# Two modulation products moved to ScalarE and GpSimd, and the weight stream put in another order

## The chip, the cores and the metric

The kernel runs on one core of a Trainium2 chip. The core has engines with a program each, which wait for one another by semaphores: TensorE (PE in the profile; PEld is its weight load), VectorE (DVE), ScalarE (ACT), GpSimd (POOL) and SyncE (SP), which issues the DMA transfers. The metric is the device time of one execution in microseconds (us), as the median of three runs.

## The reference

Two blocks of a transformer are computed in f32 for 256 tokens of width 1024. Only the start of the first block bears on this change. Each half layer is modulated by a vector c:

```python
def ada_modulation(c, w, b):
    m = jax.nn.silu(c) @ w + b            # w: 1024 x 3072
    shift, scale, gate = jnp.split(m[:, None, :], 3, axis=-1)
    return shift, scale, 1.0 + gate
...
shift, scale, gate = ada_modulation(c, ada_w[layer, 0], ada_b[layer, 0])
h = x * (1.0 + scale) + shift
y = mixer_ab(h, ...)                      # a window attention and an indexed (top-64) attention
x = layer_norm(DN_ALPHA * x + gate * y, ...)
shift, scale, gate = ada_modulation(c, ada_w[layer, 1], ada_b[layer, 1])
h = x * (1.0 + scale) + shift
y = squared_relu_mlp(h, ...)
```

So the first gate is needed when mixer_ab is done, and the shift and scale of the second half layer directly after the first layer norm.

## The kernel before, in words

All weights pass through one stream (class Stream): a list of items, mostly 128 x 2048 f32 (1 MB), which SyncE loads in the order of the list into four `raw` buffers, up to three items ahead. An item is then worked off in pieces, which the program puts between the other work (`pump`, `need`, `get`). A weight item's pieces split it into a high part `whi` (ScalarE, L157) and a low part `wlo` (VectorE, L158). An item of modulation weights has two pieces of 128 x 1024. `S.hold(key, a, b, behind)` lets the pieces of some items be issued only behind a named instruction, here the last one of `select`.

The first half layer (mixer_ab) goes as follows. VectorE makes shift and scale of the first half layer (items ada00). TensorE projects the tokens; VectorE adds up index scores for two tiles t of 128 tokens (index_scores: seven L913 steps of 128 x 128 for t = 0, seven of 128 x 256 for t = 1). `select` finds the 64 best keys of each query by rounds of MAX8 (L925) and MATCH_REPLACE8 (L928), and makes a mask of them (L933 to L947). The attention units follow, first six with that mask (ub), then six with the window mask (ua): scores on TensorE (L490, L496), a maximum on VectorE (L498), exponentials on ScalarE (L509), a division on VectorE (L526), a transpose (L534, L536) and the product with the values. The output projection by `ab_w_out` (items about) ends in the layer norm, whose inverse root is taken on GpSimd (L258).

The first gate (items ada00g) is made on TensorE: `ada_products` multiplies 32 equal columns of silu(c) with four strips of 256 columns, eight times over (L444), into one PSUM bank, and `ada_gate` adds the bias and spreads the row over the partitions (L452, L457, L459). Shift and scale of the second half layer (items ada (1, 0) to (1, 7)) are made on VectorE: sixteen multiplications of 128 x 1024 with a summed output (`ada_piece`, L436; tile junk).

The order of the instructions on each engine is fixed when the program is built, by the program's own order and a scheduler; each engine then works through its list in that order and waits at an instruction that isn't ready.

Of the kernel before, what the change touches and what calls it, by code (L numbers as in the profile page):

```python
# [8 lines left out]
F32 = DT.float32  # L9
# [4 lines left out]
AF = mybir.ActivationFunctionType  # L14
# [5 lines left out]
KT = 8  # L20
# [176 lines left out]
class Kern:  # L197
# [241 lines left out]

    def ada_products(self, raw, ps, kt, o, n):  # L440

        def pc():
            for g in range(4):
                self.nc.tensor.matmul(ps()[32 * g:32 * g + 32, 0:n], self.ccol[:, kt, :],  # L444
                                      raw[:, o + g * n:o + g * n + n], start=kt == 0, stop=kt == KT - 1)
        return pc

    def ada_gate(self, ps, gate):

        nc = self.nc  # L450
        row = self.pa.tile([128, 256], F32, tag="grow", name="grow", bufs=1)
        nc.vector.scalar_tensor_tensor(row, ps[:, 0:256], 1.0, self.gate_b, op0=ALU.add, op1=ALU.add)  # L452
        for h in range(2):
            p = self.ps("o")
            for q in range(2):
                g = 32 * (2 * h + q)
                nc.tensor.matmul(p[:, q * 256:q * 256 + 256], self.ident[:, g:g + 1].to_broadcast([128, 128]),  # L457
                                 row, start=True, stop=True)
            nc.scalar.activation(gate[:, h * 512:h * 512 + 512], p, AF.Copy, scale=1.0 / ALPHA)  # L459
# [295 lines left out]
    def mixer_ab(self, gate, early):  # L755
# [3 lines left out]
        for i in range(2):  # L759
# [8 lines left out]
        nc.scalar.activation(e, self.col("c", 0, 8), AF.Sigmoid)  # L768
        self.ccol = self.pa.tile([128, KT, 32], F32, tag="ccol", name="ccol")
        nc.gpsimd.tensor_tensor(self.ccol, self.col("c", 0, 8)[:, :, None].to_broadcast([128, KT, 32]),  # L770
                                e[:, :, None].to_broadcast([128, KT, 32]), op=ALU.mult)
        self.gate_b = self.pa.tile([128, 256], F32, tag="gate_b", name="gate_b")

# [12 lines left out]
        for kt in range(KT):  # L786
# [19 lines left out]
            for t in range(2):  # L806
                k = kt % 4
                self.mm(p0[t][:, :456], (xT[:, kt, t * 128:t * 128 + 128],), wt, slice(k * 456, k * 456 + 456),
                        kt == 0, kt == KT - 1)

        cqT = self.pa.tile([128, 2, 256], F32, tag="cqT", name="cqT", bufs=1)
# [30 lines left out]
        def ropeT(src, qT, name):  # L842
# [9 lines left out]
            return qT  # L852

        def keysT(src, kT):

            nc.gpsimd.memset(kT[0:64, :, 1, :], 0.0)
            nc.gpsimd.memset(kT[64:128, :, 0, :], 0.0)
            p = self.ps("o")
            for j in range(2):
                for t in range(2):  # L860
                    nc.tensor.transpose(p[:, j * 256 + t * 128:j * 256 + t * 128 + 128],
                                        src[t][:, j, :, :].rearrange("p a d -> p (a d)"), self.ident)
            for r in range(2):
                hs = slice(64 * r, 64 * r + 64)
                nc.scalar.activation(kT[hs, :, r, :], p[hs, :].rearrange("p (a b) -> p a b", a=2), AF.Copy)
# [9 lines left out]
        for t in range(2):  # L875
# [7 lines left out]
            iw.append(w_)  # L883
        kTb = self.px.tile([128, 2, 2, 256], F32, tag="tm", name="kTb", bufs=8)
        keysT(kd, kTb)
        iqT = self.px.tile([128, 4, 256], F32, tag="tm", name="iqT", bufs=8)
# [119 lines left out]
        self.cst_late()  # L1006
        for g in range(4):
            nc.sync.dma_start(self.gate_b[32 * g:32 * g + 32, :],
                              A["rows"][ROWS["gate_b"]:ROWS["gate_b"] + 1, 256 * g:256 * g + 256].to_broadcast([32, 256]))
        for t in range(2):  # L1010
            select(t, sc[t])
        S.hold(("ada00g", 0), 4, 16, [self.sel_last[1]])
        acc = [[None, None], [None, None]]

        kTa = self.px.tile([128, 2, 2, 256], F32, tag="tm", name="kTa", bufs=8)
        aqT = qTs[:, 0:4, :]

# [38 lines left out]
        def hook(i):  # L1056
            if i == 0:
                window()
                S.need(S.index["ada00g", 3])
            if i == 5:  # L1060
                self.ada_gate(self.strips, gate)
            if i == 11:
# [557 lines left out]
    def schedule_items(self):  # L1620
# [14 lines left out]

        def strips():

            if self.strips is None:
                self.strips = self.ps("acc")
            return self.strips  # L1640
        self.strips = None

        def gate0(j):
            def fn(raw):
                return [self.ada_products(raw, strips, 2 * j + q, 1024 * q, 256) for q in range(2)]
            S.add(("ada00g", j), A["ada"][8 + j], 2048, fn=fn)

        def ada(i, j):
            acc, mod = self.adas[i]

            def fn(raw):
                if j < 8:
                    ps = [self.ada_piece(raw, 0, acc, j), self.ada_piece(raw, 1, acc, 8 + j)]
                else:
# [7 lines left out]
        for j in range(4):  # L1662
            gate0(j)
        for j in range(4):
            S.add(("about", (j + 2) % 4), A["ab_w_out"][(j + 2) % 4], 2048, f32=j >= 2)
            ada(1, 2 * j)
            ada(1, 2 * j + 1)
        ex = {}
# [295 lines left out]
```

## Time and profile before

| | us |
|---|---|
| median of 3 runs | 1337.09 (1335.97 to 1338.56) |
| the profiled execution | 1336.42 |
| its span, from first to last instruction | 1334.5 |
| index scores and select | 52.2 to 78.7 |
| the ub units up to the fifth exponential | 81.0 to 98.9 |
| the rest of mixer_ab | 98.9 to 134.5 |
| inverse roots of the first layer norm | from 142.56 and from 152.29 |
| the first one of the second layer norm | from 331.73 |

The page gives busy times of each engine, the chain of waits that ended last, and the costliest groups of instructions. Times in rows are microseconds from the span's start; a duration in a row of the timeline includes a start-up that overlaps the instruction before it, so consecutive VectorE instructions may overlap by some 0.07 us. An f32 matmul shows as two rows.

### The profile page before, as it was taken

How to read it: one execution, taken by the hardware profiler on the slowest of the kernel's cores; microseconds unless marked ns; L12 is line 12 of the kernel's file. 1: busy time of each engine (PE TensorE's matmuls, PEld its weight loads, DVE VectorE, ACT ScalarE, POOL GpSimd, SP SyncE). 2: the span in 40 equal slices, each digit the busy share in tenths (PEclk: the TensorE clock that was granted, in tenths of full speed). 3: DMA queues.
4: the chain of work that ended last, by engine and by line, in shares of the span. 5: the costliest groups of instructions: out<-in, count | busy, mean ns of one | idle time of the engine just before them, and what ended most of it. 6: DMA issues, size and time to landing. Idle time of an engine off the chain costs nothing.

```text
span 1334.5 us, 18965 instructions
## 1 busy us (share of the span) xinstructions
PE 1289.8 (97%) x6970; PEld 1051.4 (79%) x6970; DVE 1006.6 (75%) x2048; ACT 708.1 (53%) x1532; POOL 43.8 (3%) x74
## 2 busy tenths in 40 slices
PE   5899999999999999999999999999999999999997
PEld 2356688888787788888699988888888877888886
DVE  7789999976999698666798778666677555766664
ACT  3245645554566665555543437555566754755552
POOL 2000000000100000000010000000000000000000
PEclk9999999999999999999999999999999999999999
DMA  9639689974457468555343334555534333455530
GB/s 363 252 146 332 248 299 347 343 272 158 180 202 281 158 217 300 188 191 178 109 158 116 138 127 170 188 185 188 189 139 158 126 127 126 174 189 189 190 127 32
DMA packets 39023, 260.21 MB, mean 195 GB/s; under 512 B 4625, under 2 KB 5009, under 8 KB 9362
## 3 DMA queue, kind: packets, MB, share of 16 engines
q1 hardware_dynamic: 38786, 258.47, 53.8%
q8 instruction: 55, 0.90, 0.3%
q0 software_dynamic: 144, 0.52, 0.1%
q14 instruction: 38, 0.31, 0.1%
HBM read 257.93 MB, written 1.05 MB: 194 GB/s over the span
## 4 chain that ended last, share of the span: by engine, by line
PE 73%; issue 11%; DVE 8%; ACT 3%; DMA 3%; POOL 2%; SPq 0%; POOLq 0%; DVEq 0%; ACTq 0%
PE acc L229 11%; PE acc L227 11%; PE acc L228 11%; PE scr L250 6%; PE o L250 6%; PE scr L251 3%; PE o L251 3%; PE scr L496 3%; PE acc L234 2%; DVE wlo L158 2%; DMA raw<-in_ada_dram 2%; PE o L534 1%; PE scr L229 1%; DVE junk L436 1%; POOL sm L258 1%
## 5 line engine op out<-in xcount | busy, mean ns | idle before, releaser
L158 DVE TENSOR_TENSOR wlo<-raw,whi 128x512 fp32r<-128x512 f32 x724 | 471.2, 686 | 129.8 <-ACT whi L157 119.9
L157 ACT ACTIVATE whi<-raw 128x512 fp32r<-128x512 f32 x724 | 418.9, 626 | 211.3 <-PE acc L229 87.7
L227 PE MATMUL acc<-whi,hh 128*128 128x512 f32 x512 | 201.2, 394 | 0.0
L228 PE MATMUL acc<-wlo,hh 128*128 128x512 f32 x512 | 201.2, 393 | 0.0
L229 PE MATMUL acc<-whi,hl 128*128 128x512 f32 x512 | 200.1, 392 | 0.0
L250 PE MATMUL scr<-xT,whi 128*128 128x512 f32 x464 | 166.8, 398 | 0.0
L250 PE MATMUL o<-xT,whi 128*128 128x512 f32 x464 | 166.1, 397 | 0.0
L251 PE MATMUL o<-xT,wlo 128*128 128x256 f32 x464 | 130.5, 281 | 0.0
L251 PE MATMUL scr<-xT,wlo 128*128 128x256 f32 x464 | 130.4, 281 | 0.0
L227 PEld LDWEIGHTS acc<-whi,hh 128*128 128x128 f32 x512 | 96.2, 188 | 22.9 <-ACT hh L737 1.3
L229 PEld LDWEIGHTS acc<-whi,hl 128*128 128x128 f32 x512 | 96.2, 188 | 22.1 <-DVE hl L738 0.8
L436 DVE SCALAR_TENSOR_TENSOR junk<-raw,csil 128x1024 bf16<-128x1024 f32 x88 | 108.6, 1234 | 6.2 <-DMA raw<-in_ada_dram 5.8
L228 PEld LDWEIGHTS acc<-wlo,hh 128*128 128x128 f32 x512 | 96.2, 188 | 18.6
L250 PEld LDWEIGHTS o<-xT,whi 128*128 128x128 f32 x464 | 87.1, 188 | 21.0
L250 PEld LDWEIGHTS scr<-xT,whi 128*128 128x128 f32 x464 | 87.1, 188 | 20.7 <-issue 0.5
L251 PEld LDWEIGHTS scr<-xT,wlo 128*128 128x128 f32 x464 | 87.5, 189 | 2.7 <-issue 0.5
L251 PEld LDWEIGHTS o<-xT,wlo 128*128 128x128 f32 x464 | 87.6, 189 | 0.0
L737 ACT ACTIVATE hh<-f 128x512 fp32r<-128x512 f32 x58 | 36.7, 633 | 86.8 <-DVE f L736 86.7
L731 ACT ACTIVATE r<-scr 128x256 f32<-128x256 f32 x58 | 22.3, 384 | 96.6 <-PE scr L251 96.6
L732 DVE TENSOR_TENSOR r<-scr,r 128x256 f32<-128x256 f32 x58 | 24.6, 424 | 55.7 <-ACT r L731 55.4
L738 DVE TENSOR_TENSOR hl<-f,hh 128x512 fp32r<-128x512 f32 x58 | 40.1, 691 | 33.3 <-ACT hh L737 33.1
L229 PE MATMUL acc<-whi,xT 128*128 128x512 f32 (+1 forms) x176 | 63.4, 361 | 0.7 <-DVE xT L306 0.5
(398 smaller groups left out, 2294.9 us busy)
## 6 DMA issues: line engine op xcount, KB each, us to landing
raw<-in_m_w_dram SPq DMA_DIRECT2D x128, 1024.0 KB, 4.8
raw<-in_ada_dram SPq DMA_DIRECT2D x48, 1024.0 KB, 5.4
raw<-in_c_qk_dram SPq DMA_DIRECT2D x8, 1024.0 KB, 4.9
raw<-in_h_qf_dram SPq DMA_DIRECT2D x8, 1024.0 KB, 4.8
raw<-in_mla_o_dram SPq DMA_DIRECT2D x8, 1024.0 KB, 4.8
raw<-in_c_v_dram SPq DMA_DIRECT2D x4, 1024.0 KB, 4.7
raw<-in_c_w_out_dram SPq DMA_DIRECT2D x4, 1024.0 KB, 4.8
raw<-in_h_i_dram SPq DMA_DIRECT2D x4, 1024.0 KB, 5.0
```

The source lines that it names most:

```text
L157: nc.scalar.activation(hi, raw[:, a:b], AF.Copy)
L158: nc.vector.tensor_tensor(lo, raw[:, a:b], hi.bitcast(F32), op=ALU.subtract)
L227: mm(ps, xh, wh, start=start, stop=False)
L228: mm(ps, xh, wl, start=False, stop=False)
L229: mm(ps, xl, wh, start=False, stop=stop)
L234: self.nc.tensor.matmul(ps, x[0], w(c), start=start, stop=stop)
L250: mm(ps.rearrange("p (a b) -> p a b", a=2), w.h(c), x, start=start, stop=False)
L251: mm(ps[:, n:2 * n], w.l(c), x[:, 0, :], start=False, stop=stop)
L436: nc.vector.scalar_tensor_tensor(junk, raw[:, j * 1024:(j + 1) * 1024], 1.0, self.csil, op0=ALU.mult, op1=ALU.mult, accum_out=acc[:, n:n + 1])
L496: nc.tensor.matmul(o, q, k, start=False, stop=(i == len(ops) - 1))
L737: nc.scalar.activation(hh, f, AF.Copy)
L738: nc.vector.tensor_tensor(hl, f, hh.bitcast(F32), op=ALU.subtract)
```

## The change

The first gate: ScalarE multiplies each 1 MB half by a column of silu(c) (128 x 1024, tile prod, two buffers), and GpSimd adds the product to the tile gate, eight times. `gate` starts as 1/32 on 32 partitions and zero elsewhere, with the bias loaded into its first row. Two matmuls with a matrix of ones sum it over the partitions. The TensorE strips, their PSUM bank and the VectorE step of `ada_gate` go.

The second half layer's shift and scale: GpSimd multiplies (128 x 1024, into the same two buffers prod), and ScalarE sums along the row. The sixteen L436 instructions of VectorE for items ada (1, 0) to (1, 7) go; those of other layers stay.

The stream's order: the eight items ada (1, j) now come directly after the gate's four and ahead of the four about items, where they were interleaved before. The hold begins at the first about item. The memsets of the key tiles are issued earlier.
```diff
-    def ada_products(self, raw, ps, kt, o, n):
+    def ada_rows(self, raw, kts):
+        nc = self.nc
+        def piece(q, kt):
+            def pc():
+                w = self.prod[kt % 2]
+                nc.scalar.activation(w, raw[:, q * 1024:q * 1024 + 1024], AF.Identity, scale=self.ccol[:, kt:kt + 1])
+                nc.gpsimd.tensor_tensor(self.grow, self.grow, w, op=ALU.add)
+            return pc
+        return [piece(q, kt) for q, kt in enumerate(kts)]
+
+    def ada_piece2(self, raw, j, acc, n):
+        nc = self.nc
         def pc():
-            for g in range(4):
-                self.nc.tensor.matmul(ps()[32 * g:32 * g + 32, 0:n], self.ccol[:, kt, :],
-                                      raw[:, o + g * n:o + g * n + n], start=kt == 0, stop=kt == KT - 1)
+            w = self.prod[j]
+            nc.gpsimd.tensor_tensor(w, raw[:, j * 1024:(j + 1) * 1024], self.csil, op=ALU.mult)
+            nc.scalar.activation(w, w, AF.Copy, accum_out=acc[:, n:n + 1])
         return pc
-    def ada_gate(self, ps, gate):
-        row = self.pa.tile([128, 256], F32, tag="grow", name="grow", bufs=1)
-        nc.vector.scalar_tensor_tensor(row, ps[:, 0:256], 1.0, self.gate_b, op0=ALU.add, op1=ALU.add)
+    def ada_gate(self, gate):
         for h in range(2):
             p = self.ps("o")
-            for q in range(2):
-                g = 32 * (2 * h + q)
-                nc.tensor.matmul(p[:, q * 256:q * 256 + 256], self.ident[:, g:g + 1].to_broadcast([128, 128]),
-                                 row, start=True, stop=True)
+            nc.tensor.matmul(p, self.ones, self.grow[:, h * 512:h * 512 + 512], start=True, stop=True)
             nc.scalar.activation(gate[:, h * 512:h * 512 + 512], p, AF.Copy, scale=1.0 / ALPHA)
...
+        self.grow = gate
+        self.prod = [self.pa.tile([128, 1024], F32, tag="prod", name="prod"), self.tm("prod")]
+        for a, b, v in ((0, 32, 0.0), (32, 64, 1.0 / 32), (64, 128, 0.0)):
+            nc.gpsimd.memset(gate[a:b, :], v)
...
-        S.hold(("ada00g", 0), 4, 16, [self.sel_last[1]])
+        S.hold(("about", 2), 0, 16, [self.sel_last[1]])
...
+        S.need(S.index["ada00g", 3])
...
-                S.need(S.index["ada00g", 3])
+            if i == 3:
+                S.need(S.index["ada", 1, 7])
             if i == 5:
-                self.ada_gate(self.strips, gate)
+                self.ada_gate(gate)
...
-                    ps = [self.ada_piece(raw, 0, acc, j), self.ada_piece(raw, 1, acc, 8 + j)]
+                    f = self.ada_piece2 if i == 1 else self.ada_piece
+                    ps = [f(raw, 0, acc, j), f(raw, 1, acc, 8 + j)]
...
+        for j in range(8):
+            ada(1, j)
         for j in range(4):
             S.add(("about", (j + 2) % 4), A["ab_w_out"][(j + 2) % 4], 2048, f32=j >= 2)
-            ada(1, 2 * j)
-            ada(1, 2 * j + 1)
```

Three places show what moves. On GpSimd, between the memsets of the key tile kTa and the two inverse roots of the first layer norm (L258), nothing stood before:
```order
L258 TENSOR_TENSOR sm_317<-rsq_318,mhalf 128x1
L856 MEMSET kTa 64x2x256
L857 MEMSET kTa 64x2x256
L258 TENSOR_TENSOR sm_1284<-rsq_1285,mhalf 128x1
L258 TENSOR_TENSOR sm_1339<-rsq_1340,mhalf 128x1
```

Now the eight additions to gate and the sixteen multiplications with csil (silu(c) spread over the partitions) stand there, the first and the last of each shown:
```order
L869 MEMSET kTa 64x2x256
L448 TENSOR_TENSOR gate<-gate,prod 128x1024
L448 TENSOR_TENSOR gate<-gate,prod_171 128x1024
...
L448 TENSOR_TENSOR gate<-gate,prod_171 128x1024
L458 TENSOR_TENSOR prod<-raw_607,csil 128x1024
L458 TENSOR_TENSOR prod_171<-raw_607,csil 128x1024
...
L458 TENSOR_TENSOR prod_171<-raw_804,csil 128x1024
L258 TENSOR_TENSOR sm_1270<-rsq_1271,mhalf 128x1
L258 TENSOR_TENSOR sm_1325<-rsq_1326,mhalf 128x1
```

GpSimd's twenty-four new instructions all stand ahead of the layer norm's inverse roots, and they take prod's two buffers in turn.

On ScalarE, from the last index scores (rl) to the first exponentials (pt), the list before was:
```order
L907 ACTIVATE rl_455<-scr_453 128x512
L907 ACTIVATE rl_461<-scr_459 128x512
L851 ACTIVATE hT<-o_491 128x4x128
L851 ACTIVATE hT<-o_503 128x4x128
L509 ACT_TABLE_LOAD
L509 ACTIVATE pt_613,sm_614<-scr_605,sm_611 128x128 x4
```

Now (from the same index scores on; adaacc is the sum's column):
```order
L923 ACTIVATE rl_463<-scr_461 128x512
L447 ACTIVATE prod<-raw_340,ccol 128x1024
L447 ACTIVATE prod_171<-raw_340,ccol 128x1024
...
L459 ACTIVATE prod,adaacc_89<-prod 128x1024
L459 ACTIVATE prod_171,adaacc_89<-prod_171 128x1024
...
L864 ACTIVATE hT<-o_493 128x4x128
L864 ACTIVATE hT<-o_505 128x4x128
L459 ACTIVATE prod_171,adaacc_89<-prod_171 128x1024
L459 ACTIVATE prod,adaacc_89<-prod 128x1024
L518 ACT_TABLE_LOAD
L518 ACTIVATE pt_633,sm_634<-scr_625,sm_631 128x128 x4
L459 ACTIVATE prod_171,adaacc_89<-prod_171 128x1024
```

Five sums (L459), each of which waits for a GpSimd multiplication, now stand ahead of the first exponentials, and the sixth directly behind them.

On ScalarE around the fifth ub unit's exponentials (pt_818 before, pt_853 now), before and then now:
```order
L536 ACTIVATE pT_801<-o_796 128x512
L509 ACTIVATE pt_788,sm_789<-scr_781,sm_786 128x256 x2
L272 ACTIVATE oT_807<-o_776 128x4x128
L509 ACTIVATE pt_818,sm_819<-scr_811,sm_816 128x256 x2
L536 ACTIVATE pT_831<-o_826 128x512
```

```order
L459 ACTIVATE prod,adaacc_89<-prod 128x1024
L545 ACTIVATE pT_836<-o_831 128x512
L459 ACTIVATE prod_171,adaacc_89<-prod_171 128x1024
L459 ACTIVATE prod,adaacc_89<-prod 128x1024
L272 ACTIVATE oT_842<-o_760 128x4x128
L459 ACTIVATE prod_171,adaacc_89<-prod_171 128x1024
L518 ACTIVATE pt_853,sm_854<-scr_846,sm_851 128x256 x2
```

The last of the sixteen sums stands directly ahead of the fifth unit's exponentials, so eleven of them lie between the first and the fifth unit's. The split of the about weights (L157), which before stood between the first exponentials and the fifth (four instructions), comes behind the sixth.

## Rows read from the trace of the kernel before

**Rows 1.** The page, part 1: busy us of each engine, share of the span, instructions.

```profile
PE 1289.8 (97%) x6970; PEld 1051.4 (79%) x6970; DVE 1006.6 (75%) x2048; ACT 708.1 (53%) x1532; POOL 43.8 (3%) x74
```

**Rows 2.** Busy time by stretch: stretch, us, each engine's busy us, PEclk, DMA share, GB/s.

```profile
52.20:78.70 26.50, 26.21 (x81) 12.75 (x80) 25.33 (x90) 4.50 (x8) 0.00 (x0) 1.00 0.06 21
81.00:98.90 17.90, 15.69 (x124) 9.57 (x123) 14.64 (x45) 12.14 (x42) 0.00 (x0) 1.00 0.66 265
98.90:134.50 35.60, 35.60 (x207) 22.90 (x206) 33.43 (x98) 20.25 (x67) 0.00 (x0) 1.00 0.90 327
```

**Rows 3.** The chain of waits, two pieces in order of time: start, us, what.

```profile
84.32 5.34 DMA raw<-in_ab_w_out_dram
...
174.43 8.36 DMA raw<-in_m_w_dram
```

**Rows 4.** Timeline at index scores, mask, exponentials' table, fifth unit: start, us, instruction, [idle before, releaser].

```profile
51.28 0.60 ACT L907 ACTIVATE rl<-scr 128x512 f32<-128x512 f32 x1 [1.28 <-PE scr L903]
...
78.34 0.43 DVE L947 CAST smask<-eq 128x512 bf16<-128x512 f32 x1
...
79.65 1.28 ACT L509 ACT_TABLE_LOAD   x1 [3.56 <-DVE sm L501]
...
98.89 0.49 ACT L509 ACTIVATE pt<-scr,sm 128x256 f32<-128x256 f32 x1
```

**Rows 5.** GpSimd's timeline, same columns.

```profile
142.56 0.86 POOL L258 TENSOR_TENSOR sm<-rsq,mhalf 128x1 f32<-128x1 f32 x1 [100.49 <-DVE rsq L257]
...
197.57 2.72 POOL L470 TENSOR_TENSOR diag<-cst,adamod 128x1024 f32<-128x1024 f32 x1 [44.73 <-DVE adamod L463]
331.73 0.55 POOL L258 TENSOR_TENSOR sm<-rsq,mhalf 128x1 f32<-128x1 f32 x1 [131.44 <-DVE rsq L257]
...
342.97 1.89 POOL L470 TENSOR_TENSOR diag<-cst,adamod 128x1024 f32<-128x1024 f32 x1
...
514.66 2.13 POOL L470 TENSOR_TENSOR diag<-cst,adamod 128x1024 f32<-128x1024 f32 x1 [45.62 <-DVE adamod L463]
```

**Rows 6.** ScalarE's groups, whole program: busy us, mean ns of one | idle before, releasers.

```profile
L1200 ACT ACTIVATE sqj<-h 128x1024 f32<-128x1024 f32 x6 | 6.4, 1073 | 0.0
```

**Rows 7.** VectorE's timeline beside those three L470, and the same lines elsewhere.

```profile
143.46 0.55 DVE L588 TENSOR_SCALAR r<-r,sm,sm 128x512 f32<-128x512 f32 x1 [0.44 <-POOL sm L258]
...
197.31 1.22 DVE L436 SCALAR_TENSOR_TENSOR junk<-raw,csil 128x1024 bf16<-128x1024 f32 x1
...
198.79 2.58 DVE L436 SCALAR_TENSOR_TENSOR junk<-raw,csil 128x1024 bf16<-128x1024 f32 x1
...
201.30 0.68 DVE L736 SCALAR_TENSOR_TENSOR f<-r 128x512 f32<-128x512 f32 x1
...
343.03 2.11 DVE L588 TENSOR_SCALAR r<-r,sm,sm 128x512 f32<-128x512 f32 x1 [0.44 <-POOL sm L258]
...
514.95 2.39 DVE L736 SCALAR_TENSOR_TENSOR f<-r 128x512 f32<-128x512 f32 x1
```

**Rows 8.** VectorE's groups from 52.2 to 78.7, columns as in rows 6.

```profile
L913 DVE SCALAR_TENSOR_TENSOR isc<-rl,iw,isc 128x256 f32<-128x256 f32 x7 | 3.3, 477 | 0.1
...
L913 DVE SCALAR_TENSOR_TENSOR isc<-rl,iw,isc 128x128 f32<-128x128 f32 x7 | 2.5, 352 | 0.3
...
L422 DVE TENSOR_TENSOR bq<-rpa,rpb 128x512 f32<-128x512 f32 x2 | 1.4, 679 | 0.0
...
L937 DVE TENSOR_TENSOR_SCAN cum<-eq,zero 128x256 f32<-128x256 f32 x1 | 0.7, 692 | 0.0
...
L941 DVE TENSOR_TENSOR gt<-cum,gt 128x128 f32<-128x128 f32 x1 | 0.3, 279 | 0.0
```

**Rows 9.** ScalarE's groups from 52 to 135, columns as in rows 6.

```profile
L536 ACT ACTIVATE pT<-o 128x512 f32<-128x512 f32 x12 | 7.3, 604 | 12.2 <-PE o L534 12.1
...
L157 ACT ACTIVATE whi<-raw 128x512 fp32r<-128x512 f32 x10 | 6.0, 655 | 0.8 <-DMA raw<-in_ab_w_out_dram 0.8
```

**Rows 10.** TensorE's groups of the first gate, columns as in rows 6.

```profile
L444 PE MATMUL acc<-raw,ccol 128*32 128x256 f32 x64 | 4.7, 385 | 0.0
```

More of the change, by code (lines that the diff above doesn't have):

```diff
@@ L768, in mixer_ab @@
         nc.scalar.activation(e, self.col("c", 0, 8), AF.Sigmoid)
[L769 to L772, printed above, removed]
+        self.ccol = self.pa.tile([128, KT], F32, tag="ccol", name="ccol")
+        nc.gpsimd.tensor_tensor(self.ccol, self.col("c", 0, 8), e, op=ALU.mult)
+        self.grow = gate
+        self.prod = [self.pa.tile([128, 1024], F32, tag="prod", name="prod"), self.tm("prod")]
+        for a, b, v in ((0, 32, 0.0), (32, 64, 1.0 / 32), (64, 128, 0.0)):
+            nc.gpsimd.memset(gate[a:b, :], v)
         self.adab = self.p1.tile([128, 96], F32, tag="adab", name="adab")
@@ L809, in mixer_ab @@
                         kt == 0, kt == KT - 1)
+        nc.sync.dma_start(gate[0:1, :], A["rows"][ROWS["gate_b"]:ROWS["gate_b"] + 1, :])
         cqT = self.pa.tile([128, 2, 256], F32, tag="cqT", name="cqT", bufs=1)
@@ L852, in ropeT, with keys_zero, keysT @@
             return qT
-        def keysT(src, kT):
+        def keys_zero(kT):
             nc.gpsimd.memset(kT[0:64, :, 1, :], 0.0)
             nc.gpsimd.memset(kT[64:128, :, 0, :], 0.0)
+        def keysT(src, kT):
             p = self.ps("o")
@@ L884, in mixer_ab @@
         kTb = self.px.tile([128, 2, 2, 256], F32, tag="tm", name="kTb", bufs=8)
+        keys_zero(kTb)
         keysT(kd, kTb)
@@ L1006, in mixer_ab @@
         self.cst_late()
-        for g in range(4):
-            nc.sync.dma_start(self.gate_b[32 * g:32 * g + 32, :],
-                              A["rows"][ROWS["gate_b"]:ROWS["gate_b"] + 1, 256 * g:256 * g + 256].to_broadcast([32, 256]))
         for t in range(2):
             select(t, sc[t])
-        S.hold(("ada00g", 0), 4, 16, [self.sel_last[1]])
+        S.hold(("about", 2), 0, 16, [self.sel_last[1]])
         acc = [[None, None], [None, None]]
         kTa = self.px.tile([128, 2, 2, 256], F32, tag="tm", name="kTa", bufs=8)
+        keys_zero(kTa)
+        S.need(S.index["ada00g", 3])
         aqT = qTs[:, 0:4, :]
@@ L1634, in schedule_items @@
         S.add(("abin", 2, 0), A["ab_in2"], 2048, f32=True)
[L1636 to L1641, printed above, removed]
         def gate0(j):
             def fn(raw):
-                return [self.ada_products(raw, strips, 2 * j + q, 1024 * q, 256) for q in range(2)]
+                return self.ada_rows(raw, (2 * j, 2 * j + 1))
             S.add(("ada00g", j), A["ada"][8 + j], 2048, fn=fn)
```

## The prediction, made before the changed kernel ran

> **What bounds the kernel now.** I read the page's busy line first: TensorE is busy for 97% of the span, VectorE 75%, ScalarE 53%, GpSimd 3% [rows 1]. Over the whole program GpSimd looks free. The change sits in mixer_ab alone, so I then read busy time by stretch, and there it looks different [rows 2]. From 52.2 to 78.7, in the index scores and `select`, TensorE is busy for 26.21 of 26.50 us, but VectorE also for 25.33: it has 1.17 us to spare, while ScalarE works for 4.50 and GpSimd not at all. From 81.0 to 98.9 ScalarE works for 12.14 of 17.90 us. From 98.9 to 134.5 TensorE is busy throughout and VectorE for 33.43 of 35.60. The chain of waits runs, behind `select`, through a load of the about weights (84.32, 5.34 us) [rows 3]. `select` ends with the second mask at 78.34, just ahead of the first exponentials, whose table is loaded at 79.65 after a wait for VectorE [rows 4]. The layer norm's inverse root at 142.56 is a good mark for the end of the stage, the next one at 331.73 for the end of the MLP [rows 5]. If the two marks move by the same amount, the MLP gave nothing back.
>
> **GpSimd's work, and what it costs by itself.** The change gives GpSimd 24 two-input instructions of 128 x 1024. The nearest rows are three L470 of that size, at 1.89, 2.13 and 2.72 us [rows 5]. I take 1.89, the one that had its inputs at hand: 24 x 1.89 = 45.4 us. The first addition needs a first product. ScalarE's first rl runs from 51.28 to 51.88 [rows 4], and a 128 x 1024 activation takes 1.07 us, by six L1200 [rows 6]. So GpSimd begins at about 53 and could end at 98.4. Now it does nothing for 100.49 us ahead of 142.56 [rows 5], so it looks as if all of it were hidden.
>
> **What it collides with.** The same three L470 show otherwise when VectorE's rows beside them are read [rows 7]. The L436 that starts at 198.79, while the first L470 runs (197.57 to 200.29), takes 2.58 us; its neighbour takes 1.22. L588 at 343.03, beside the second, takes 2.11 us, and 0.55 at 143.46. L736 at 514.95, beside the third, takes 2.39, and 0.68 at 201.30. Each ends about when a start at the end of the L470 would make it end: VectorE stood still until GpSimd was done. The other way round the first L470 is 0.83 us longer than the second, about what was left of the L436 that began at 197.31. So the two engines take turns in such instructions.
>
> [...]
>
> **Term 1, index scores and select.** In the 26.5 us from 52.2, VectorE runs 26 instructions with two SBUF inputs: fourteen L913 (3.3 + 2.5 us), two L422 (1.4), and two each of L916, L937, L940, L941 and L945 (0.28 to 0.69 us each; I take 3.8 for the ten) [rows 8], together 11.0 us. The other 14.3 us lie between them, 0.55 us per gap on average. When GpSimd always has work, each of its instructions starts in a gap and stops VectorE for 1.89 - 0.55 = 1.34 us. How many meet VectorE there? The new order on ScalarE puts sums 1 to 5 ahead of the first exponentials and the sixth behind them. GpSimd's eighth multiplication overwrites what the sixth sum reads, so GpSimd can do 8 additions and 7 multiplications, 15 instructions, before the exponentials have run, and these wait for `select`. 15 x 1.34 = 20.1 us. Some of the 15 will fall into the rounds of MAX8 and MATCH_REPLACE8, which have one input, and cost nothing there: I take off one and a half of them and use 18. The ends: 0, if the short instructions slip past, and 15 x 1.89 = 28.4 if each is waited out whole. No row shows a collision with an L913 or a scan itself; 18 lies near the three that are shown.
>
> Without collisions the five sums would delay nothing: the thirteenth GpSimd instruction would end at 53 + 13 x 1.89 = 77.6, its sum at about 78.7, ahead of the table load at 79.65.
>
> **Term 2, the ub units.** Eleven sums now stand on ScalarE between the first and the fifth unit's exponentials, which today lie 81.0 to 98.9 [rows 2, 4]. A sum takes 1.07 us, like L1200, which has the shape and the summed output too [rows 6]. So 11 x 1.07 = 11.8 us come in, and four L157 of 0.655 us, 2.6, go out [rows 9]: 12.14 + 11.8 - 2.6 = 21.3 us of work where there are 17.9. The least is +3.4, with no idle time left. If ScalarE keeps its idle 5.8 us (it waits for TensorE and VectorE in the same places) it is +9.2. GpSimd has nine multiplications left for this stretch, 17.0 us, one after the other with a sum between, and collides with L422 and the divisions L526; the most would be +17.0, if nothing lay beside them. I take 8: the load of the about weights at 84.32, which holds ScalarE's list up today, no longer stands ahead of the exponentials, and pays for some of the collisions.
>
> **Term 3, from the fifth unit to the layer norm.** VectorE loses sixteen L436 (1.22 us, 19.5 in all), most of them after 98.9. ScalarE waits there mostly for L534 on TensorE, 12.1 us from 52 to 135 [rows 9], some of which stands behind a division that stood behind an L436. Between nothing and -12.1, if each of these waits did, I take -2, since TensorE is busy throughout the stretch. The four moved L157 come in here again, beside TensorE.
>
> **Costed at nothing.** TensorE loses 64 rows of L444 (4.7 us) [rows 10], and the two matmuls with ones take the place of the four that spread the row. The cover is that it would then stand and wait for the exponentials, which come later than before; without that cover it would be a gain of nearly 5. Three memsets of gate on GpSimd before 10 us, and a 4 KB load of the bias, have some 28 us until GpSimd's next use. On SyncE the gate's four loads keep their place, and ada (1, 0) follows as soon as ScalarE has read a raw tile; the first load of the MLP waits for the multiplication four raw items earlier, well ahead of its use at 134.
>
> **Sum.** 18 + 8 - 2 = 24 us at the layer norm's mark. After it the order of work is the old one, and TensorE carries the MLP, so nothing gives it back. The profiled execution took 1336.4, which makes 1360.4. The median of the runs is 0.7 above that execution: 1361.
>
> **The rivals.**
> *The collision spares the short instructions* (term 1 is 0): 1337.1 + 8 - 2 = 1343. For it: the rows show only VectorE instructions of 512 columns or more being held. Against it: nothing in them depends on the length, and L588 was held with a single large input.
> *GpSimd is slower on plain SBUF operands than in L470*, whose inputs are broadcast. With its longest row, 2.72 us, term 1 is 13.5 x (2.72 - 0.55) = 29, the nine multiplications 24.5 instead of 17.0, term 2 about 15: 1337.1 + 29 + 15 - 2 = 1379. Against it: 0.83 of the 2.72 was a wait.
> [...]
> *The stream gets ahead* (the other side: faster). The DMA queues stand idle from 52.2 to 78.7 (21 GB/s) [rows 2], because the raw tiles wait for TensorE's strips. ScalarE frees them sooner now. If terms 1 and 2 come to no more than the 3 us that ScalarE's idle can hide, and the wait of 8.36 us for MLP weights at 174.43 [rows 3] goes, the result is 1337 - 8 = 1329. It decides only if neither engine is delayed, and four raw buffers limit how far ahead a load can run.
> *Nothing moves*: terms 1 and 2 near their lower ends, 3.4, against -2 to -5 in term 3: 1337.
>
> **Chances.** The forecast has 60% with its own range 1351 to 1371; the spared short instructions 15%; a slower GpSimd 13%; faster 6%; no change 6%. A change within 0.2%, 2.7 us, can't be told from none here. So faster 0.06, same 0.06, slower 0.88. The range from 1342 to 1375 leaves out the two cases below and the upper half of the slower GpSimd.
>
> **What would show it.** In the new profile L448 (x8) and L458 (x16) should take about 1.9 us each, and index-score steps (L929, now L913) more than 1 us on average instead of 0.352 and 0.477. The second mask (L963) should come 15 to 22 us later than its 78.34, the fifth unit's exponentials near 125, the first layer norm's inverse root near 167, the second's near 356. ScalarE should wait for GpSimd ahead of L459. If L929 keeps its 0.35 us, term 1 is wrong. If the mark at 142.56 moves and the one at 331.73 doesn't, the claim that nothing is given back is wrong.

## The result: 37.8 us slower, and the profile after

The changed kernel takes 1374.31 us (1373.65 to 1374.79, 4 runs), the kernel before 1336.53 beside it (4 runs): +37.8 us, a ratio of 1.0282 with a 95% interval of 1.027 to 1.0295. The forecast was 1361 with a range of 1342 to 1375, so the sign and the range hold, but the forecast time was 13.3 us short and its own range (1351 to 1371) was missed.

The page's busy line of the changed kernel answers to [rows 1]. VectorE is shown busy for 25 us more, although sixteen L436 (19.5 us) were taken from it:

```profile
PE 1289.0 (94%) x6895; PEld 1051.9 (77%) x6902; DVE 1031.6 (75%) x2015; ACT 734.4 (54%) x1572; POOL 103.1 (8%) x101
```

Busy time by stretch, columns as in [rows 2]. The stretches are cut at the same places of the program: from the first index scores to the second mask, from there to the fifth unit's exponentials, and the rest of mixer_ab.

```profile
53.90:104.00 50.10, 26.58 (x77) 14.89 (x76) 48.99 (x86) 18.78 (x26) 35.55 (x15) 0.80 0.43 147
104.00:137.40 33.40, 17.50 (x71) 10.64 (x70) 28.42 (x45) 23.07 (x61) 21.64 (x9) 0.74 0.54 191
137.40:172.00 34.60, 33.55 (x193) 21.66 (x193) 23.86 (x80) 28.03 (x82) 0.00 (x0) 0.95 0.43 156
```

The first stretch grew from 26.5 to 50.1 us, and VectorE seems busy for 48.99 of it, with 86 instructions where there were 90. TensorE runs 77 instructions where it ran 81, in twice the time.

The timeline answers to [rows 4 and 5]: the second mask, the table, the fifth unit, and the inverse roots of the two layer norms.

```profile
103.55 0.43 DVE L963 CAST smask<-eq 128x512 bf16<-128x512 f32 x1
...
104.86 1.28 ACT L518 ACT_TABLE_LOAD   x1 [12.58 <-DVE sm L510]
...
137.39 0.46 ACT L518 ACTIVATE pt<-scr,sm 128x256 f32<-128x256 f32 x1
...
180.50 0.55 POOL L258 TENSOR_TENSOR sm<-rsq,mhalf 128x1 f32<-128x1 f32 x1 [44.20 <-DVE rsq L257]
...
368.88 0.55 POOL L258 TENSOR_TENSOR sm<-rsq,mhalf 128x1 f32<-128x1 f32 x1 [131.42 <-DVE rsq L257]
```

Against before the mask is 25.2 us late, the fifth unit 38.5, the first layer norm 37.9, the second 37.2. The loss is made in two places, 25.2 and 13.3 us, and the MLP gives back under a microsecond.

GpSimd's own timeline shows the 24 new instructions, in runs (the last five of them left out):

```profile
55.63 4.76 POOL L448 TENSOR_TENSOR gate<-gate,prod 128x1024 f32<-128x1024 f32 x2 [13.25 <-issue]
62.41 2.42 POOL L448 TENSOR_TENSOR gate<-gate,prod 128x1024 f32<-128x1024 f32 x1 [2.02 <-ACT prod L447]
66.99 12.35 POOL L448 TENSOR_TENSOR gate<-gate,prod 128x1024 f32<-128x1024 f32 x5 [2.15 <-ACT prod L447]
79.30 16.44 POOL L458 TENSOR_TENSOR prod<-raw,csil 128x1024 f32<-128x1024 f32 x7
108.77 9.38 POOL L458 TENSOR_TENSOR prod<-raw,csil 128x1024 f32<-128x1024 f32 x4 [13.03 <-ACT prod L459]
```

One takes 16.44 / 7 = 2.35 us from start to start, not 1.89. As predicted, 15 of them run before the exponentials, then GpSimd waits 13.03 us for the sixth sum.

And VectorE's timeline in the tail of `select`, while GpSimd works back to back (its instructions begin 2.35 us apart from 79.30, at 84.0, 86.3, 88.7, 91.0):

```profile
81.76 0.33 DVE L949 TENSOR_SCALAR_CACHE_REDUCE gt<-isc,sm 128x128 f32<-128x128 f32 x1
...
82.01 2.08 DVE L951 TENSOR_SCALAR eq<-isc,sm 128x128 f32<-128x128 f32 x1
...
84.14 0.40 DVE L944 MATCH_REPLACE8 mr<-sm,isc 128x256 f32<-128x256 f32 x1
84.47 2.12 DVE L953 TENSOR_TENSOR_SCAN cum<-eq,zero 128x128 f32<-128x128 f32 x1
86.51 0.40 DVE L941 MAX8 sm<-mr 128x8 f32<-128x256 f32 x1
86.83 2.05 DVE L956 SCALAR_TENSOR_TENSOR cum<-cum,sm,eq 128x128 f32<-128x128 f32 x1
...
91.50 2.02 DVE L960 TENSOR_SCALAR eq<-gt 128x128 f32<-128x128 f32 x1
```

Every second instruction lasts about 2 us, and each ends a tenth or two behind the start of a new GpSimd instruction. MAX8, MATCH_REPLACE8 and the tensor-scalar that also sums (L949) pass in 0.33 to 0.40. Here VectorE gets one instruction of the kind that can be stopped (2.02 to 2.12 us) for each one of GpSimd (2.35 from start to start). In the chain of waits from 50 to 185 us this reads as VectorE's own work, and GpSimd isn't among the lines shown; nor does the profile list any wait of VectorE for another engine from 53.9 to 104:

```profile
by line: DVE isc L929 14.1%; DVE pt L535 7.9%; PE acc L234 7.0%; PE scr L505 5.1%; DVE mr L944 3.9%; PE o L543 3.8%; PE o L558 3.8%; DVE sm L941 3.6%; PE acc L228 2.9%; DVE sm L510 2.8%; PE acc L227 2.7%; PE acc L229 2.7%; DVE kr L422 2.5%;
```

In the units short instructions grow as well. From 104 to 137.4 the divisions (L535), the products L422 and the small scalings L510 show:

```profile
L535 DVE TENSOR_SCALAR pt<-pt,sm 128x128 f32<-128x128 f32 x8 | 6.0, 805 | 0.0
L535 DVE TENSOR_SCALAR pt<-pt,sm 128x256 f32<-128x256 f32 x4 | 5.5, 1417 | 0.0
L422 DVE TENSOR_TENSOR kr<-rpa,rpb 128x128 f32<-128x128 f32 x2 | 3.5, 1728 | 0.0
L510 DVE TENSOR_SCALAR sm<-sm 128x2 f32<-128x2 f32 x4 | 2.3, 569 | 0.1
```

Before, one division took 0.28 and 0.35 us, such an L422 0.29 and such a scaling 0.16.

### The profile page after: what moved, and what is told of

The parts are those of the page before. It is cut to its first block, busy times and chain, and to the rows that moved or that the text cites. A ratio compares the mean times of both kernels' runs of the same rounds, so it can differ in the third digit from the quotient of the medians.

```text
span 1371.9 us, 18858 instructions
## 1 busy us (share of the span) xinstructions
PE 1289.0 (94%) x6895; PEld 1051.9 (77%) x6902; DVE 1031.6 (75%) x2015; ACT 734.4 (54%) x1572; POOL 103.1 (8%) x101
## 3 DMA queue, kind: packets, MB, share of 16 engines
q1 hardware_dynamic: 38596, 258.34, 52.2%
## 4 chain that ended last, share of the span: by engine, by line
PE 79%; DVE 13%; ACT 3%; DMA 2%; POOL 1%; issue 1%; SPq 0%; DVEq 0%; POOLq 0%; ACTq 0%
PE acc L227 12%; PE acc L229 12%; PE acc L228 12%; PE o L250 8%; PE scr L250 8%; PE o L251 4%; PE scr L251 4%; PE scr L505 2%; DMA raw<-in_ada_dram 2%; DVE isc L929 1%; PE o L543 1%; POOL sm L258 1%; DVE wlo L158 1%; PE acc L1364 1%; PE scr L229 1%
## 5 line engine op out<-in xcount | busy, mean ns | idle before, releaser
L157 ACT ACTIVATE whi<-raw 128x512 fp32r<-128x512 f32 x724 | 418.8, 626 | 214.7 <-PE acc L229 88.7
L258 POOL TENSOR_TENSOR sm<-rsq,mhalf 128x1 f32<-128x1 f32 (+2 forms) x26 | 19.2, 737 | 1007.6 <-DVE rsq L257 1007.6
L436 DVE SCALAR_TENSOR_TENSOR junk<-raw,csil 128x1024 bf16<-128x1024 f32 x72 | 89.0, 1237 | 6.6 <-DMA raw<-in_ada_dram 6.3
```

The lines of the kernel that those rows point to most:

```text
L157: nc.scalar.activation(hi, raw[:, a:b], AF.Copy)
L258: nc.gpsimd.tensor_tensor(out, v, self.mhalf[:, :n], op=ALU.pow)
L436: nc.vector.scalar_tensor_tensor(junk, raw[:, j * 1024:(j + 1) * 1024], 1.0, self.csil, op0=ALU.mult, op1=ALU.mult, accum_out=acc[:, n:n + 1])
```

## The experiments

Theory A says that GpSimd's instructions stop VectorE's, and that this is the price. The rivals: GpSimd's slow work is itself late and is handed on through ScalarE's sums (B, later D), or the new order costs (C). Differences are against the median of the kernel before in the same comparison (1336.6).

### The two engines by themselves (e0_probe)

```diff
+        for i in range(4):
+            nc.gpsimd.tensor_tensor(w, a, b, op=ALU.mult)
...
+        for i in range(22):
+            nc.gpsimd.tensor_tensor(w, a, b, op=ALU.mult)
...
+        for i in range(4):
+            nc.vector.tensor_tensor(z[:, 0:128], d[:, 0:128], a[:, 128:256], op=ALU.mult)
```


> The kernel before with a probe behind its last output, which changes nothing of what is computed. GpSimd runs four products each of 128 x 1024, of 128 x 512, of 128 x 1024 with broadcast inputs (the inputs of L470), and four one-input scalings of 128 x 1024, with VectorE idle; then 22 products of 128 x 1024 while VectorE runs short instructions of six kinds. Theory A (turns: a GpSimd instruction stops VectorE's instructions of some kinds until it ends): alone, GpSimd takes 2.34 us, 1.2 us, 1.9 us for the first three, and beside it VectorE's 128 x 128 products, f32 scalings and 128 x 1024 products end only with a GpSimd instruction, one for each (1.5 to 2.4 us instead of 0.3), while MAX8 keeps its 0.28 us. Theory B (GpSimd's own work is late and is handed on through ScalarE; VectorE's waits are beside the point): GpSimd alone takes 1.9 us for plain inputs too and was stretched to 2.35 by VectorE, and VectorE's short instructions are held by less than half a microsecond.

The groups behind the last output: GpSimd's first four kinds, which ran with VectorE idle, and three of VectorE's from beside GpSimd's 22 products:

```profile
L1627 POOL TENSOR_TENSOR pw__2262_12802<-pa__2260_12800,pb__2261_12801 128x1024 f32<-128x1024 f32 x4 | 9.4, 2340 | 3.9 <-ACT pb__2261_12801 L1624 3.7
...
L1629 POOL TENSOR_TENSOR pw__2262_12802<-pa__2260_12800,pb__2261_12801 128x512 f32<-128x512 f32 x4 | 5.0, 1262 | 0.3
...
L1631 POOL TENSOR_TENSOR pw__2262_12802<-pa__2260_12800,pb__2261_12801 128x1024 f32<-128x1024 f32 x4 | 7.6, 1895 | 0.3
...
L1635 POOL TENSOR_SCALAR pw__2262_12802<-pa__2260_12800 128x1024 f32<-128x1024 f32 x4 | 11.1, 2771 | 0.3
...
L1651 DVE RECIPROCAL pz__2263_12803<-pd__2264_12804 128x128 f32<-128x128 f32 x4 | 3.8, 953 | 0.1
L1653 DVE TENSOR_REDUCE sm<-pd__2264_12804 128x4 f32<-128x512 f32 x4 | 2.7, 673 | 0.0
L1643 DVE MAX8 sm<-pd__2264_12804 128x8 f32<-128x128 f32 x5 | 1.4, 281 | 0.0
```

So 2.34 us is what two plain inputs take; L470 is shorter because its inputs are broadcast (1.895). Beside it, VectorE's products and scalings of 128 x 128:

```profile
1370.85 0.28 DVE L1643 MAX8 sm<-pd__2264_12804 128x8 f32<-128x128 f32 x1
1371.05 2.29 DVE L1645 TENSOR_TENSOR pz__2263_12803<-pd__2264_12804,pa__2260_12800 128x128 f32<-128x128 f32 x1
...
1378.23 2.29 DVE L1647 TENSOR_SCALAR pz__2263_12803<-pd__2264_12804 128x128 f32<-128x128 f32 x1
```

Theory A holds. MAX8 (0.281 us), the reduction (0.673) and the reciprocal (0.953; four in 3.8 us, less than two of GpSimd's instructions) are not stopped. A miss: the 128 x 1024 products took 3.04 us on average, not up to 2.4, since their own time, an estimated 1.2 us (an L436 of that size takes 1.22), comes on top of the wait, and GpSimd was held by them in turn (2.50 on average over its 22).

### The additions alone (e1_gate_only)

```diff
-                    f = self.ada_piece2 if i == 1 else self.ada_piece
+                    f = self.ada_piece
```


> The changed kernel with the sixteen products of items ada (1, 0) to (1, 7) back on VectorE (L436), so that GpSimd has the eight additions alone and ScalarE no sums. Theory A: eight additions of 2.35 us run inside the index scores and select; VectorE's normal stretch between two instructions that can be stopped is about 0.73 us (26.5 us, 36 such instructions), so of 18.8 us of additions 1 - 0.73 / 2.35 = 0.69 are lost: second mask 13 us later (91), and 1337 + 13 - 2 for TensorE's strips = 1346 to 1352. Theory B: no sum stands ahead of the exponentials, so nothing is late: 1333 to 1339.

1355.27 us, +18.7 (ratio 1.0125 to 1.0155; the new order is in this figure). B is out: there isn't a single sum, and the first mask is late already. The first mask comes at 84.89 instead of 70.94, 13.9 late as A says; the second is later than that (100.27), because the new order puts seven of the L436 (1.21 to 1.22 us each) between the two masks. The total was missed by 3 us for that.

### The products alone (e4_ada_only)

The kernel before with the new order and the products moved; the gate stays on TensorE's strips. Of the edit, the line that chooses is shown.

```diff
-                    ps = [self.ada_piece(raw, 0, acc, j), self.ada_piece(raw, 1, acc, 8 + j)]
+                    f = self.ada_piece2 if i == 1 else self.ada_piece
+                    ps = [f(raw, 0, acc, j), f(raw, 1, acc, 8 + j)]
```


> The other half alone: the sixteen products on GpSimd and their sums on ScalarE in the changed stream order, the gate on TensorE's strips as before. ScalarE's list has no sum ahead of the first exponentials, so two products at most run before them. Theory A: the second mask is 2 to 4 us late (81 to 82); then fourteen products of 2.35 us, each with a sum, fall into the units: the fifth unit 12 to 16 us late, 1348 to 1356 in all. Theory B: sixteen products start earlier than they are needed and GpSimd has 8 x 2.35 = 19 us less to do than in the changed kernel: 1355.

1361.38 us, +24.8 (1.0169 to 1.0203), beyond A's 1348 to 1356, and B's 1355 too. No product ran before the mask, which came at 78.41. The sixteen products, all in the units, cost 24.8 us together with the new order. In this build products and sums mostly wait for one another, so by itself it doesn't say whether stops or waits make the price; ScalarE's waits from 78 to 150 us:

```profile
ACT prod L454 <- POOL prod L453: 13.1, 12, 2.5
ACT L518 <- DVE sm L510: 4.7, 1, 4.7
```

### GpSimd's work behind select (e6_behind_select)

One tiny GpSimd instruction that reads the second mask holds back all of GpSimd's additions but the first.

```diff
         keys_zero(kTa)
+        nc.gpsimd.tensor_scalar(gate[64:128, 0:1], smask[1][64:128, 0:1], 0.0, None, op0=ALU.mult)
```


> The changed kernel with one more tiny GpSimd instruction, which reads the second mask and writes an unused zero of gate, so that all of GpSimd's additions but the first run behind select. (By that the scheduler also puts the sums behind the first exponentials.) Theory A: select is nearly free of stops: second mask near 81 instead of 103.55. GpSimd's 23 instructions of 2.35 us then lie in the units, and the fifth unit's exponentials come near 122 instead of 137: 1352 to 1365 in all, faster than the changed kernel. Theory B: GpSimd's work starts 24 us later than in the changed kernel and is late by as much more: 1385 to 1398.

1374.42 us, +37.8 (1.0271 to 1.0302): both theories missed. The mask is back at 79.64, 24 us earlier than in the changed kernel, and the end is the same. The fifth unit's exponentials come at 127.08 instead of near 122. I took this for a sign that the chain of products and sums sets the end (theory D), and tested that next.

### The order alone (e3_order_only)

The order of the list is shown; the hold and the places at which items are asked for move with it.

```diff
+        for j in range(8):
+            ada(1, j)
         for j in range(4):
             S.add(("about", (j + 2) % 4), A["ab_w_out"][(j + 2) % 4], 2048, f32=j >= 2)
-            ada(1, 2 * j)
-            ada(1, 2 * j + 1)
```


> The kernel before with nothing but the changed order of the stream and the places at which it is asked for (the sixteen products stay L436 on VectorE, the gate on TensorE's strips). Theory A (all of the change's price comes from GpSimd's instructions): 1334 to 1341. Theory C (the order itself costs, since the about weights come behind eight more items): 1345 or more.

1344.67 us, +8.0 (1.005 to 1.0092; its profile is of a run of 1350.09). It lies between the two expectations: the order costs something while VectorE still has the L436.

### The same work in shorter instructions (e5_halves)

The additions are cut in two in the same way.

```diff
-            nc.gpsimd.tensor_tensor(w, raw[:, j * 1024:(j + 1) * 1024], self.csil, op=ALU.mult)
+            for s in (0, 512):
+                nc.gpsimd.tensor_tensor(w[:, s:s + 512], raw[:, j * 1024 + s:j * 1024 + s + 512],
+                                        self.csil[:, s:s + 512], op=ALU.mult)
```


> The changed kernel with each GpSimd instruction cut into two of 128 x 512 (1.26 us each by the probe, 1.32 from start to start; 63 us in all instead of 57). Theory A (VectorE gets one instruction that can be stopped for each GpSimd instruction, so the loss goes with the length of one): of the time in which GpSimd is busy 1 - 0.73 / 1.32 = 0.45 is lost instead of 0.69: some 16 to 17 us up to the second mask, which comes near 95 instead of 103.55. If the mask's time sets the end, 1365 to 1367. Theory D (the chain of GpSimd's products and ScalarE's sums sets the end, and the mask's time is absorbed in it): the mask near 95 too, but the end 2 to 6 us later than the changed kernel, 1376 to 1381.

1368.34 us, +31.7 (1.0224 to 1.0254). The mask comes at 97.51. More time on GpSimd, less in all: A's direction, 1.3 us above its interval, and well below D's.

### Without the multiplications, and without the sums (e7_no_mult, e8_no_sum)

```diff
-            nc.gpsimd.tensor_tensor(w, raw[:, j * 1024:(j + 1) * 1024], self.csil, op=ALU.mult)
-            nc.scalar.activation(w, w, AF.Copy, accum_out=acc[:, n:n + 1])
+            nc.scalar.activation(w, raw[:, j * 1024:(j + 1) * 1024], AF.Copy, accum_out=acc[:, n:n + 1])
```


> The changed kernel without GpSimd's sixteen multiplications: ScalarE sums the raw weights instead, so shift and scale of the second half layer are not the reference's. GpSimd keeps the eight additions. Theory A: second mask 13 us late as in the kernel with the additions alone (91 to 92); ScalarE's sums cost what little its idle time doesn't hide, 2 to 6 us: 1348 to 1356. Were ScalarE's work the bound, the eleven sums in the units would show with their 11.8 us: 1358 to 1362.

```diff
-            nc.scalar.activation(w, w, AF.Copy, accum_out=acc[:, n:n + 1])
+            nc.scalar.activation(acc[:, n:n + 1], self.csil[:, n:n + 1], AF.Copy)
```


> The changed kernel without ScalarE's sixteen sums: the products are made and nobody reads them, so shift and scale of the second half layer are not the reference's, and GpSimd's 24 instructions run back to back with nobody waiting for one of the sixteen. Theory A (stops alone): GpSimd is busy from 55.6 to some 114, and VectorE goes at 0.73 / 2.35 = 0.31 of its pace all that time, so that select's last 24 us of work from 55.6 take until 115 or more: second mask 113 to 118, 1365 to 1375. Theory D (the chain of products and sums sets the end, the stops matter little): without the chain 1345 to 1352.

Without the multiplications 1351.15 us, +14.5 (1.01 to 1.0135), mask at 92.12. Without the sums 1370.45 us, +33.8 (1.0238 to 1.0268), mask at 116.64; there GpSimd runs without a pause from 68.17 on, and select stands under it to the end. Its mask and its last sixteen products:

```profile
116.64 2.45 DVE L963 CAST smask<-eq 128x512 bf16<-128x512 f32 x1
```

```profile
80.48 38.33 POOL L458 TENSOR_TENSOR prod<-raw,csil 128x1024 f32<-128x1024 f32 x16
```

All four numbers are A's (one mask by 0.1 us beyond its interval). Without the multiplications the first layer norm comes 64.7 us behind the mask, with ten of ScalarE's sixteen sums in between and no L436 on VectorE, and 64.2 before; taking the sums away saves 4 of 37.8 us. The edit between the changed kernel and the one without multiplications leaves out only these, so the sixteen cost 23.2 us.

### Behind select, without the sums (e9_behind_no_sum)

The last edit and the tiny instruction of e6_behind_select together.


> The kernel whose GpSimd work runs behind select, with ScalarE's sixteen sums left out as well, so shift and scale of the second half layer are not the reference's. Nothing on ScalarE but five products of the gate waits for GpSimd, whose 23 instructions lie in the units from 80 to some 136. Theory D (behind select it is the handing over from GpSimd to ScalarE that costs, and VectorE has slack in the units): 1345 to 1354, at least 20 us less than with the sums. Theory A (stops on VectorE cost in the units as they do in select, since the divisions of every unit are f32 scalings that can be stopped): 1364 to 1374.

1373.09 us, +36.5 (1.0258 to 1.0288). D falls: with nobody waiting for a multiplication the time is within 1.3 us of what it was with the sums. But something does wait. On ScalarE the first unit's four exponentials stand among five products of the gate, and each of these waits for a GpSimd addition to free its buffer (0.93 to 1.75 us). So they begin from 81.12 to 94.12, 13.0 us from the first to the last, where it was 1.04 before; VectorE stands idle for 8.8 us of it, waiting for them. These some 12 us are handed on by semaphores and aren't stops.

What lies behind them is stops. The divisions of the units, VectorE's groups from 80 to 142 us, first without the multiplications, then in this kernel (eight of each shape fall into the window):

```profile
L534 DVE TENSOR_SCALAR pt<-pt,sm 128x256 f32<-128x256 f32 x16 | 4.9, 349 | 0.2
L534 DVE TENSOR_SCALAR pt<-pt,sm 128x128 f32<-128x128 f32 x16 | 3.5, 282 | 0.1
```

```profile
L535 DVE TENSOR_SCALAR pt<-pt,sm 128x128 f32<-128x128 f32 x8 | 14.8, 1906 | 0.0
...
L535 DVE TENSOR_SCALAR pt<-pt,sm 128x256 f32<-128x256 f32 x8 | 10.9, 1387 | 0.0
```

Sixteen divisions take 25.7 us instead of 5. By the handing over and by these stops the work behind `select` lost what it had won in it.

### The gate alone in the old order, beside and behind select (e10_gate_old_order, e11_gate_behind)

The first is the kernel with the additions alone and this (hold and places of asking as in the kernel before too); the second has the tiny instruction of e6_behind_select as well.

```diff
-        for j in range(8):
-            ada(1, j)
         for j in range(4):
             S.add(("about", (j + 2) % 4), A["ab_w_out"][(j + 2) % 4], 2048, f32=j >= 2)
+            ada(1, 2 * j)
+            ada(1, 2 * j + 1)
```


> The gate's part of the change alone, in the stream order of the kernel before: eight additions on GpSimd, no sums, the sixteen L436 on VectorE as before and behind the second mask. Theory A: second mask 13 to 14 us late (92), the end 12 to 14 us late: 1348 to 1351. If the 6 us between the kernel with the additions alone in the new order (1355.3) and the one without multiplications (1351.2) came from the order rather than from L436 in select, 1345 to 1349.

> The same with the tiny instruction that reads the second mask ahead of GpSimd's additions 2 to 8, so that they run from 80 to 97, in the units. Theory A: the mask is 1 to 2 us late (79.6). The first unit's exponentials stand among the gate's products on ScalarE, which wait for five additions: 10 to 12 us late; the end 1345 to 1352. If the units have slack for that: 1335 to 1342, and TensorE's strips saved would then show.

1350.50 us, +13.9 (1.0091 to 1.0121), and 1350.42 us, +13.8 (1.0083 to 1.0119). Eight additions cost the same in both places, but not by the same path. The first comes out as A says, with its mask at 95.11 instead of 92 (the profile is of a run of 1352.25, and its first addition begins at 57.29, 2.5 us later than without the multiplications). In the second the mask is 1.8 us late and the first layer norm 14.7. Nearly all of the rest arises in the first unit: its exponentials stand among the gate's products again, begin from 81.27 to 95.46, and ScalarE's waits from 78 to 98 and the chain from 79 to 98 name GpSimd:

```profile
81.27 0.37 ACT L518 ACTIVATE pt<-scr,sm 128x128 f32<-128x128 f32 x1
...
87.86 0.35 ACT L518 ACTIVATE pt<-scr,sm 128x128 f32<-128x128 f32 x1
...
93.04 0.35 ACT L518 ACTIVATE pt<-scr,sm 128x128 f32<-128x128 f32 x1
...
95.46 0.35 ACT L518 ACTIVATE pt<-scr,sm 128x128 f32<-128x128 f32 x1
```

```profile
ACT prod L447 <- POOL gate L448: 7.4, 5, 2.3
```

```profile
by line: POOL gate L448 66.9%; DVE pt L535 12.0%; DVE junk L436 9.3%; issue 8.2%; DVE sm L507 3.2%; POOL gate L1030 2.8%; ACT pt L518 2.4%; DVE smask L963 2.3%; DVE gt L957 2.2%; DVE eq L961 1.4%; DVE eq L960 1.1%; DVE sm L529 0.9%; DVE sm 
```

So this run doesn't show a stop's price in the units. No kernel was run in which the additions lie among the units and the first exponentials don't stand behind them. No version beats the kernel before: in every place that was tried, GpSimd's instructions cost more than the others saved by them.

The price in one table, the difference over the number of GpSimd's new instructions. In the three rows behind select the additions cost by handing over, so their last column isn't the price of a stop:

| kernel | instructions | us slower | each |
|---|---|---|---|
| the change | 24 x 2.35 us | 37.8 | 1.57 |
| work behind select | 24 | 37.8 | 1.57 |
| behind select, no sums | 24 | 36.5 | 1.52 |
| no sums | 24 | 33.8 | 1.41 |
| products alone | 16 | 24.8 | 1.55 |
| additions alone, old order | 8 | 13.9 | 1.74 |
| the same behind select | 8 | 13.8 | 1.73 |
| no multiplications | 8 | 14.5 | 1.81 |
| the change against no multiplications | 16 | 23.2 | 1.45 |
| halves | 48 x 1.26 us | 31.7 | 0.66 |

Where it costs by stops, an instruction costs its length less 0.5 to 0.9 us, which is about what VectorE does between two instructions that can be stopped (0.73 us in select, an estimate from 26.5 us and 36 such instructions before).

## Why the prediction was right, and where its terms were off

*The mechanism of term 1 was right.* The two engines take turns, shown by the probe (VectorE's 128 x 128 product took 0.27 us just ahead of GpSimd's products and 2.22 to 2.29 beside them), by the lengths in select (2.02 to 2.12 us) and in the units (0.805 and 1.417 for a division instead of 0.28 and 0.35), and by the halves (31.7 us instead of 37.8). The gap of VectorE's free work, 0.55 us in the prediction, is 0.5 to 0.9 by the table. That the range held is near to luck: the time lies 0.7 us below its end, both main terms were too small, and what term 2 counted isn't what cost.

*Term 1 was 25.2 instead of 18.* The step that failed is "I take 1.89" for GpSimd's instruction. It was read from L470, whose inputs are broadcast; plain inputs take 2.34. With it the prediction's own formula gives 13.5 x (2.35 - 0.55) = 24.3. The rows also had 2.13 and 2.72, and the difference in the inputs was seen and then left to a rival. That rival, a slower GpSimd, named the cause; it was priced at 1379 with 2.72. The count of 15 instructions ahead of the exponentials was right. That the 26 instructions with two SBUF inputs are the ones to count, and that MAX8 and MATCH_REPLACE8 cost nothing, was the author's estimate: no row of the kernel before shows it. In the runs one-input f32 scalings are stopped as well: of 128 x 128, L951 took 2.08 us, L960 2.02 and L1647 1.90 to 2.29. L949, the one that also sums, took 0.33, and beside GpSimd MATCH_REPLACE8 took 0.27 to 0.41 us and MAX8 0.28 to 0.43.

*Term 2 was 13.3 instead of 8, and for another reason than the one given.* The prediction counted ScalarE's eleven sums, 11.8 us of work. Without the multiplications the stage behind the mask takes 64.7 us with most of the sums in it, against 64.2 before, so the sums cost next to nothing there. What the trace shows in their place is VectorE held by the nine multiplications left: by the lengths above and those of L422's and L510's other shapes, the divisions take 8.5 us more than before, L422 3.8 and L510 3.1, together some 15 us. ScalarE waited for a product four times, 3.9 us in all, off the chain of waits. The price of the sixteen, 1.45 us each, makes 13 us for nine. This cost was named ("collides with L422 and the divisions"), but not priced.

*Term 3 was -0.6 instead of -2*, and nothing was given back in the MLP (-0.8), as forecast. What VectorE gains by sixteen L436 less can't be told apart from what the new order and the sums cost: with all three and eight additions it is +14.5, with the additions alone in the old order +13.9.

*The marks.* L448 and L458 took 2.35 us where 1.9 was forecast; L929 1.85 us (128 x 256) and 0.94 (128 x 128) where over 1 was; the mask 25.2 us late where 15 to 22 was; the fifth unit at 137.4 instead of 125; the layer norms at 180.5 and 368.9 instead of 167 and 356. Of the rivals the spared short instructions are out (L951 of 128 x 128 waits as long as any), and so is the stream that gets ahead, since its condition failed: terms 1 and 2 came to 38.5 us and not to 3.

*Open:* TensorE's granted clock was 0.80 and 0.74 on average in the two stretches, where it was 1.00 before, while TensorE was busy for about half of the time (26.58 of 50.10 us and 17.50 of 33.40); what part of the 37.8 us this has was not measured. By the chain of waits it is small: that has no TensorE work from 53.9 to 104, and 2.3 us of it from 104 to 137.4. Why the order alone costs 8 us, and how much of that is in the 37.8, was not followed up.

## What to carry to other kernels

GpSimd wasn't a spare engine here, beside a VectorE that is on the path: its products and additions of 128 x 1024 in SBUF held those VectorE instructions with two SBUF inputs that were measured beside them (index-score steps, scans, products), and its f32 scalings, until they ended (0.2 to 0.4 us became 1.9 to 2.3 for 128 x 128 in select and in the probe). A later place gained nothing (37.8 us in both), partly by the same stops and partly because ScalarE's exponentials then stood behind products that waited for GpSimd. Price stops as (number of instructions) x (length - VectorE's free work between two such instructions), with a length measured for the same kind of inputs, and if it must be there, cut it short (31.7 us instead of 37.8 in halves). In a profile look for short VectorE instructions that take as long as GpSimd's and end when one of those ends: the waits and the chain didn't name this, and the busy time counted it as work. A handing over by semaphores they do name, as behind `select`; look for both.

## What the runs showed of the hardware that was not expected

- With broadcast inputs GpSimd's 128 x 1024 product took 1.895 us, with plain ones 2.340; the scaling with one plain input took longer than either, 2.771.
- VectorE's rope products that read one input from PSUM kept their length while GpSimd worked (L417 of 128 x 512, 0.67 and 0.68 us in the changed kernel, 0.68 before); the one from SBUF behind them (L422) took 1.46 to 2.0 us there in three of four and 1.38 to 1.59 behind `select` in three of four, instead of 0.69 or less. A copy under a mask (L932, 2.23 us instead of 0.29) and the cast of the mask (2.22 and 2.45 us where the sums are left out, instead of 0.42) are stopped too.
- The turns are lopsided: in the changed kernel GpSimd's instructions stayed between 2.34 and 2.48 us in select, while VectorE's of 128 x 128 went from 0.3 to 2.1.
